# Three-pass projections of a decoder step: the products with the low weight parts moved behind the others within a chunk

## The chip, the cores and the metric

One NeuronCore of a Trainium2 chip runs the whole program; the other cores are idle. The metric is the device time of one execution in microseconds (us), lower is better. TensorE (PE in the rows) multiplies into PSUM; ScalarE (ACT), VectorE (DVE) and GpSimdE (POOL) do the elementwise work; SyncE (SP) issues the DMAs.

## What is computed

One inference step of a small two-layer decoder, for 1024 prompt tokens and 8 x 4 sample tokens together (1056 columns). The part of the reference that matters here, cut:

```python
# layer 0 (self path)
h, s_fin = _hgrn2(_rmsnorm(x, a_norm), a_w_in, lbs, a_out_norm, a_w_out, state0, chunk, sub)
x = x + h
x = x + jnp.square(relu(_rmsnorm(x, mlp_norm[0]) @ mlp_w_up[0])) @ mlp_w_down[0]
# layer 1 (cross path)
kv = _rmsnorm(x, kv_norm) @ w_kv            # keys get a per-head norm and a rotary
q = _rmsnorm(x, b_norm) @ b_w_q             # 3 groups x 8 heads, the same norm and rotary
o = merge of three dilated attentions over (q, kv), weighted by their softmax denominators
x = x + o @ b_w_o
x = x + jnp.square(relu(_rmsnorm(x, mlp_norm[1]) @ mlp_w_up[1])) @ mlp_w_down[1]
```

`_hgrn2` projects q, f, i and og with `a_w_in` (1024 x 4096) and runs a gated recurrence with a 128 x 128 state per head.

## The kernel before

Everything is float32, and TensorE multiplies in its float32r form. Each operand of a product is held as a high part (`whi` for weights, `opH` for activations) and a low part, what is left of the value (`wlo`, `opL`). A product of weights and activations is three matmuls into the same PSUM bank: high x high (HH), high weight x low activation (HL), low weight x high activation (LH).

**Weights.** `weight_order` lists all weight tiles (128 x 1024 each) in the order of their use. `_prep` (lines 125 to 163) loads one with two DMAs of 256 KB into `wraw`; ScalarE copies each half into `whi` (L131), and GpSimdE subtracts it for `wlo` (L132). For the key, value and query weights GpSimdE first multiplies by a gain (L148). `whi` and `wlo` have two buffers each, so a tile's split waits until TensorE has done with the tile two before it. `wnext` prepares one tile ahead.

**Projections.** `mm3` (lines 180 to 189) is the helper of all projections but the MLP's second half (`mmx`, not touched). For one output tile of 128 rows and one chunk of columns it issues, for each of 8 blocks of the contraction (4 in the output projections), HH (L185), HL (L186) and LH (L187):

```python
for i, (kw, kx) in enumerate(ks):
    nc.tensor.matmul(ps, wh[:, kw, :], xh[:, kx, :], start=(i == 0), stop=False)
    nc.tensor.matmul(ps, wh[:, kw, :], xl[:, kx, :], start=False, stop=False)
    nc.tensor.matmul(ps, wl[:, kw, :], xh[:, kx, :], start=False, stop=(i == len(ks) - 1))
    if self.fine and 2 * i + 2 == len(ks):
        self.tick()
```

`proj_n` goes over three chunks (352 columns each in the first layer's mixer and the attention stage, 384, 384 and 288 elsewhere) and calls `mm3` and the evacuation of the bank, for one weight tile or, in the first projection and the first of the attention stage, for two in turn. `tick` lets one piece of a recurrence or an attention generator issue its instructions, after each chunk and, where `fine` is set, at half a chunk; so their small matmuls stand among the products. The order on each engine is that of a scheduler, which starts from the program's order and priorities (`high_priority`) and pulls forward what it takes to be ready.

**The start.** The input norm runs chunk by chunk (`norm`, lines 250 to 282): squares and their sum, a matmul with ones (L273), the reciprocal root on ScalarE (L239, L240), then for each of 8 blocks a multiply on VectorE (L281), the high part on ScalarE (L232) and the low part on GpSimdE or VectorE (L233). The first projection (f and q of head 0, banks `pj_226` and `pj_354` for chunk 0) follows it block by block.

**The attention stage.** `unit` projects a key tile (its squares on ScalarE, L1040, are summed by a matmul with ones, L1042), a value tile and four query tiles, for each of 2 x 3 units; attention runs between. Afterwards come the output projection and the second MLP.

Of the kernel before, what the change touches and what calls it, by code (L numbers as in the profile page):

```python
# [46 lines left out]
class Kern:  # L47
    def __init__(self, nc, tc, aps, ctx):
        self.nc, self.tc, self.a, self.ctx = nc, tc, aps, ctx
        self.const = ctx.enter_context(tc.tile_pool(name="const", bufs=1))  # L50
        self.rs = ctx.enter_context(tc.tile_pool(name="rs", bufs=2))
        self.op = [self.const.tile([P, KD, NT], F32R, name=n) for n in ("opH", "opL")]
        self.chunks = CHUNKS
        self.wp = ctx.enter_context(tc.tile_pool(name="wp", bufs=2))
        self.pp = ctx.enter_context(tc.tile_pool(name="pp", bufs=4, space=PSUM))
        self.pg = ctx.enter_context(tc.tile_pool(name="pg", bufs=4, space=PSUM))
        self.wx = None
        self.wt = {}
        self.wi = 0
        self.wq = self.weight_order()  # L60
        self.queue, self.lanes = deque(), []
        self.merged = 0
        self.every, self.ticks = 0, 0
        self.rawx = False
        self.fine = False

    def bank(self):
        return self.pg.tile([P, 512], F32, name="g")
# [111 lines left out]
    def mm3(self, ps, w, x, ks):  # L180

        nc = self.nc
        (wh, wl), (xh, xl) = w, x
        for i, (kw, kx) in enumerate(ks):
            nc.tensor.matmul(ps, wh[:, kw, :], xh[:, kx, :], start=(i == 0), stop=False)  # L185
            nc.tensor.matmul(ps, wh[:, kw, :], xl[:, kx, :], start=False, stop=False)  # L186
            nc.tensor.matmul(ps, wl[:, kw, :], xh[:, kx, :], start=False, stop=(i == len(ks) - 1))  # L187
            if self.fine and 2 * i + 2 == len(ks):
                self.tick()

    K8 = [(k, k) for k in range(KD)]
# [134 lines left out]
    def phase_a(self):  # L326
        nc, tc, a = self.nc, self.tc, self.a
# [38 lines left out]
        def ev_to(t):  # L366
            def ev(c, ps):
                with hp():
                    nc.scalar.activation(t[:, c * CW:(c + 1) * CW], ps, AF.Copy)
            return ev  # L370

        def sigmoid(x, mul):

            for c in range(NCH):
                x_ = x[:, c * CW:(c + 1) * CW]
                n = gp.tile([P, CW], F32, name="sg")
                nc.scalar.activation(n, x_, AF.Abs)
                nc.scalar.activation(n, n, AF.Exp, scale=-1.0)
                nc.scalar.activation(n, n, AF.Ln, bias=1.0)
                o = n if mul else x_  # L380
                nc.vector.scalar_tensor_tensor(o, x_, 0.0, n, op0=ALU.min, op1=ALU.subtract)
                nc.scalar.activation(o, o, AF.Exp)
                if mul:
                    nc.vector.tensor_tensor(x_, x_, n, op=ALU.mult)

        def ev_f(h, b, kt, lf):
            def ev(c, ps):
                sl = slice(c * CW, (c + 1) * CW)
                with hp():
                    f = gp.tile([P, CW], F32, name="fr")  # L390
                    nc.scalar.activation(f, ps, AF.Copy)
                n = gp.tile([P, CW], F32, name="fn", bufs=1)
                nc.scalar.activation(n, f, AF.Abs)
                nc.scalar.activation(n, n, AF.Exp, scale=-1.0)
                nc.scalar.activation(n, n, AF.Ln, bias=1.0)
                nc.vector.scalar_tensor_tensor(lf[:, sl], f, 0.0, n, op0=ALU.min, op1=ALU.subtract)
                nc.vector.scalar_tensor_tensor(n, f, 0.0, n, op0=ALU.max, op1=ALU.add)
                nc.scalar.activation(kt[:, sl], n, AF.Exp, scale=-1.0, bias=self.lnlb[:, h:h + 1])
                nc.vector.tensor_scalar(f, f, -80.0, None, op0=ALU.max)
                nc.scalar.activation(f, f, AF.Exp, scale=-1.0)  # L400
                nc.scalar.activation(f, f, AF.Ln, scale=self.lb[:, h:h + 1], bias=1.0)
                nc.vector.tensor_tensor(lf[:, sl], lf[:, sl], f, op=ALU.add)
                n, off = min(CW, NP_ - c * CW), c * CW % P
                nc.vector.tensor_tensor_scan(
                    b[:, c * CW:c * CW + n], self.reset[:, off:off + n], lf[:, c * CW:c * CW + n],
                    0.0 if c == 0 else b[:, c * CW - 1:c * CW], op0=ALU.mult, op1=ALU.add)
                if n < CW:
                    nc.vector.tensor_tensor_scan(b[:, NP_:], self.reset[:, 448:], lf[:, NP_:], 0.0, op0=ALU.mult, op1=ALU.add)

                for i in ((), (2, 3), (6, 7))[c]:  # L410
                    s = slice(i * P, i * P + P)
                    nc.vector.scalar_tensor_tensor(b[:, s], lf[:, s], b[:, s.stop - 1:s.stop], b[:, s], op0=ALU.add, op1=ALU.subtract)
            return ev

        def gate(h, og):
            self.proj(self.wnext(), ops, ev_to(og))
            sigmoid(og, False)
            nc.gpsimd.tensor_copy(self.so[:, h, :], og[:, NP_:])

        self.fine = True  # L420
        for h in range(8):
            b = gp.tile([P, NT], F32, name="b")
            kt = gp.tile([P, NT], F32, name="k")
            q = gp.tile([P, NT], F32, name="q")
            lf = gp.tile([P, NT], F32, name="lf", bufs=1)
            if h == 0:
                w = [self.wnext(), self.wnext()]
                self.proj_n(w, ops, [ev_f(h, b, kt, lf), ev_to(q)])
                for i in range(4):
                    mt = gp.tile([P, 512], F32, name="lv", bufs=6)[:, :480]  # L430
                    nc.sync.dma_start(mt, a["masks"][:, 480 * i:480 * i + 480])
                    nc.vector.tensor_copy(self.masks[:, 480 * i:480 * i + 480], mt)
            else:
                gate(h - 1, og)
                self.proj(self.wnext(), ops, ev_f(h, b, kt, lf))
                self.proj(self.wnext(), ops, ev_to(q))
            sigmoid(q, True)
            vT = gp.tile([P, NT], F32, name="vT", bufs=1)
            self.proj(self.wnext(), ops, ev_to(vT))
            if h % 4 == 0:  # L440
                new = [gp.tile([P, 4, NS], F32, name=f"s_{n}", bufs=1) for n in "bkqv"]
            for d, s in zip(new, (b, kt, q, vT)):
                nc.gpsimd.tensor_copy(d[:, h % 4, :], s[:, NP_:])
            og = gp.tile([P, NT], F32, name="og", bufs=1)
            self.queue.append(self.gla(h, b, kt, q, vT, og))
            if h == 3:
                self.lanes.append(self.gla_sample(0, new))
# [1074 lines left out]
```

## Time and profile before

| | |
|---|---|
| median of 3 runs | 2947.27 us (2946.01 to 2949.76) |
| the profiled execution's own time | 2947.01 us |
| its span | 2945.2 us |
| TensorE busy | 2853.4 us, 97% |
| VectorE / ScalarE / GpSimdE busy | 56% / 45% / 44% |
| moved by DMA | 201.90 MB, 69 GB/s on average |
| stages, about | recurrence to 620 us, MLP to 1415, attention and output to 2180, MLP to the end |

Matmuls overlap in the profile: a row's duration is longer than the distance to the next one's start. Waits in brackets are idle time just before an instruction, and what ended it.

### The profile page before, as it was taken

The numbers are of one execution on the slowest core, as the hardware profiler recorded it, in microseconds if no ns is written. First come the engines' busy times: TensorE is split into PE (matmuls) and PEld (weight loads), VectorE is DVE, ScalarE is ACT, GpSimd is POOL, SyncE is SP. The second block draws the span as 40 slices with busy tenths as digits, with TensorE's granted clock in tenths as the row PEclk, the third lists the DMA queues.
The fourth block names the chain that finished last, engine by engine and source line by source line (L and its number), as shares of the span: only waits on it lengthen the run. The fifth ranks groups of instructions, "written<-read, shape, count | busy, mean of one in ns | idle before, by whom it ended". The sixth has DMA issues, their size and how long they took to land.

```text
span 2945.2 us, 47177 instructions
## 1 busy us (share of the span) xinstructions
PE 2853.4 (97%) x18144; PEld 2747.6 (93%) x18144; DVE 1663.9 (56%) x3353; ACT 1330.1 (45%) x3045; POOL 1308.9 (44%) x1119
## 2 busy tenths in 40 slices
PE   6999999999999999999899999999999999999999
PEld 6999899889999999999889889889889999999999
DVE  8777777864454445443745555665675454444442
ACT  6676667743333322332445545555544233333221
POOL 5444454542554445453564454333214454544442
PEclk9999999999999999999999999999999999999999
DMA  3111211230111111112312234332651111111112
GB/s 117 38 31 37 74 38 34 88 102 29 51 44 51 44 51 47 48 51 70 94 44 77 73 102 119 127 116 70 196 165 44 51 44 50 51 44 50 44 51 88
DMA packets 131954, 201.90 MB, mean 69 GB/s; under 512 B 26321, under 2 KB 65873, under 8 KB 129681
## 3 DMA queue, kind: packets, MB, share of 16 engines
q1 hardware_dynamic: 131728, 198.88, 21.7%
q8 instruction: 143, 2.34, 0.3%
q14 instruction: 83, 0.67, 0.1%
HBM read 164.04 MB, written 34.80 MB: 68 GB/s over the span
## 4 chain that ended last, share of the span: by engine, by line
PE 60%; POOL 10%; DVE 7%; DMA 5%; issue 5%; ACT 3%; POOLq 0%; DVEq 0%; ACTq 0%; SPq 0%
PE pj L185 11%; PE pj L186 11%; PE pj L187 11%; POOL wlo L132 5%; PE pj L853 4%; PE pj L854 4%; PE pj L855 4%; DMA wraw<-w_dn 4%; POOL wlox L132 2%; PE g L854 2%; PE g L853 2%; PE g L855 2%; PE g L1195 2%; PE g L1167 2%; PE g L1182 1%
## 5 line engine op out<-in xcount | busy, mean ns | idle before, releaser
L185 PE MATMUL pj<-opH,whi 128*128 128x352 f32 (+2 forms) x3408 | 1134.7, 333 | 6.0 <-ACT opH L232 3.5
L186 PE MATMUL pj<-opL,whi 128*128 128x352 f32 (+2 forms) x3408 | 1107.2, 325 | 1.6 <-POOL opL L233 1.3
L187 PE MATMUL pj<-opH,wlo 128*128 128x352 f32 (+2 forms) x3408 | 1102.9, 324 | 3.0 <-POOL wlo L132 2.7
L132 POOL TENSOR_TENSOR wlo<-wraw,whi 128x512 fp32r<-128x512 f32 x404 | 546.4, 1372 | 976.6 <-ACT whi L131 939.8
L185 PEld LDWEIGHTS pj<-opH,whi 128*128 128x128 f32 x3408 | 644.6, 189 | 24.7 <-issue 13.7
L186 PEld LDWEIGHTS pj<-opL,whi 128*128 128x128 f32 x3408 | 645.3, 189 | 11.4 <-issue 5.2
L187 PEld LDWEIGHTS pj<-opH,wlo 128*128 128x128 f32 x3408 | 644.2, 189 | 7.0 <-POOL wlo L132 4.2
L131 ACT ACTIVATE whi<-wraw 128x512 fp32r<-128x512 f32 x404 | 233.0, 622 | 561.7 <-PE g L854 442.7
L767 DVE SCALAR_TENSOR_TENSOR tmp<-pj,scale 128x384 f32<-128x384 f32 (+1 forms) x192 | 99.8, 520 | 302.8 <-PE pj L187 302.8
L867 DVE TENSOR_TENSOR xr<-xr,pj 128x384 f32<-128x384 f32 x336 | 184.4, 552 | 143.4 <-PE pj L855 143.3
L768 ACT ACTIVATE tmp<-tmp 128x384 f32<-128x384 f32 (+1 forms) x192 | 94.8, 494 | 290.3 <-DVE tmp L767 289.5
L536 POOL TENSOR_TENSOR lv<-b 128x512 f32<-128x512 f32 x112 | 127.9, 1156 | 80.1 <-PE g L640 43.1
L132 POOL TENSOR_TENSOR wlox<-wsum,whix 128x512 fp32r<-128x512 f32 x112 | 151.4, 1373 | 0.0
L162 POOL TENSOR_TENSOR wsum<-wraw,wsum 128x256 f32<-128x256 f32 x56 | 41.4, 739 | 170.8 <-DVE wsum L160 166.5
L1172 ACT ACTIVATE pr<-pr,nm 128x128 f32<-128x128 f32 (+1 forms) x192 | 84.1, 440 | 65.9 <-DVE nm L1170 65.7
L1169 DVE CUSTOM_DVE_ANT_0 pr<-g,band,rq 128x128 f32<-128x128 f32 (+1 forms) x192 | 68.0, 404 | 77.2 <-PE g L1167 73.5
L148 POOL TENSOR_TENSOR wraw<-wraw,gains 128x512 f32<-128x512 f32 x72 | 92.1, 1284 | 42.2 <-DMA wraw<-w_q 34.8
L211 DVE TENSOR_TENSOR xr<-xr,pj 128x384 f32<-128x384 f32 (+1 forms) x132 | 67.5, 516 | 75.1 <-PE pj L855 38.1
L773 DVE TENSOR_TENSOR tmp<-tmp 128x384 f32<-128x384 f32 x84 | 80.5, 984 | 46.5 <-ACT tmp L768 46.5
L1019 POOL TENSOR_TENSOR q<-q,cos 32x512 f32<-32x512 f32 x48 | 89.3, 1866 | 29.8 <-DVE rsw L1018 28.5
L854 PE MATMUL g<-hL,whi 128*128 128x288 f32 x336 | 99.8, 297 | 0.0
L853 PE MATMUL g<-hH,whi 128*128 128x288 f32 x336 | 98.9, 294 | 0.0
(400 smaller groups left out, 5714.1 us busy)
## 6 DMA issues: line engine op xcount, KB each, us to landing
wraw<-w_up SPq DMA_DIRECT2D x128, 256.0 KB, 2.9
wraw<-w_dn SPq DMA_DIRECT2D x128, 256.0 KB, 2.8
wraw<-w_in SPq DMA_DIRECT2D x64, 256.0 KB, 2.8
wraw<-w_q SPq DMA_DIRECT2D x48, 256.0 KB, 3.0
ub<-us SPq DMA_DIRECT2D x32, 256.0 KB, 2.2
cc<-ck SPq DMA_DIRECT2D x8, 1024.0 KB, 4.9
cc<-cv SPq DMA_DIRECT2D x8, 1024.0 KB, 5.2
wraw<-w_kv SPq DMA_DIRECT2D x24, 256.0 KB, 2.9
```

What stands on the lines that cost most here:

```text
L131: nc.scalar.activation(hi[:, j:j + 4, :], raw, AF.Copy)
L132: nc.gpsimd.tensor_tensor(lo[:, j:j + 4, :], raw, hi[:, j:j + 4, :].bitcast(F32), op=ALU.subtract)
L185: nc.tensor.matmul(ps, wh[:, kw, :], xh[:, kx, :], start=(i == 0), stop=False)
L186: nc.tensor.matmul(ps, wh[:, kw, :], xl[:, kx, :], start=False, stop=False)
L187: nc.tensor.matmul(ps, wl[:, kw, :], xh[:, kx, :], start=False, stop=(i == len(ks) - 1))
L536: nc.gpsimd.tensor_tensor(r(lv), r(b), r(b)[:, :, h - 1:h].to_broadcast([P, 256 // h, 2 * h]), op=ALU.subtract)
L767: nc.vector.scalar_tensor_tensor(r, ps, 0.0, self.scale[c], op0=ALU.max, op1=ALU.mult)
L768: nc.scalar.activation(r, r, AF.Square)
L853: nc.tensor.matmul(ps, wh[:, kw, :], xh, start=start and i == 0, stop=False, skip_group_check=True)
L854: nc.tensor.matmul(ps, wh[:, kw, :], xl, start=False, stop=False, skip_group_check=True)
L855: nc.tensor.matmul(ps, wl[:, kw, :], xh, start=False, stop=stop and i == len(items) - 1, skip_group_check=True)
L867: self.nc.vector.tensor_tensor(x(i, c), x(i, c), ps, op=ALU.add)
```

## The change

Within one call of `mm3` the products are listed in two passes. The first has HH and HL for each block in turn; the second has LH for all blocks. The first product of the list starts the bank and the last one stops it. The tick in the middle still falls after half of the products. The attribute `fresh` is set and cleared and nothing reads it.

```diff
         (wh, wl), (xh, xl) = w, x
-        for i, (kw, kx) in enumerate(ks):
-            nc.tensor.matmul(ps, wh[:, kw, :], xh[:, kx, :], start=(i == 0), stop=False)
-            nc.tensor.matmul(ps, wh[:, kw, :], xl[:, kx, :], start=False, stop=False)
-            nc.tensor.matmul(ps, wl[:, kw, :], xh[:, kx, :], start=False, stop=(i == len(ks) - 1))
-            if self.fine and 2 * i + 2 == len(ks):
+
+        hh, hl, lh = (wh, xh), (wh, xl), (wl, xh)
+        passes = ((hh, hl), (lh,))
+        todo = [(f, kw, kx) for p in passes for kw, kx in ks for f in p]
+        for i, ((f, g), kw, kx) in enumerate(todo):
+            nc.tensor.matmul(ps, f[:, kw, :], g[:, kx, :], start=(i == 0), stop=(i == len(todo) - 1))
+            if self.fine and 2 * i + 2 == len(todo):
                 self.tick()
```

Two places of TensorE's order. In the changed program all products have line 190, the norm's matmul L273 is L276, and L1042 is L1046.

The first is in the first projection, from the product of chunk 0, block 6 on. `pj_226` and `pj_354` are chunk 0 of the two weight tiles (`whi_89` and `whi_103`), `pj_380` and `pj_421` chunk 1. Before:

```order
L185 MATMUL pj_226<-opH_61,whi_89 128x352
L186 MATMUL pj_354<-opL_62,whi_103 128x352
L187 MATMUL pj_354<-opH_61,wlo_104 128x352
L185 MATMUL pj_380<-opH_61,whi_89 128x352
L185 MATMUL pj_421<-opH_61,whi_103 128x352
L186 MATMUL pj_380<-opL_62,whi_89 128x352
L187 MATMUL pj_380<-opH_61,wlo_90 128x352
L185 MATMUL pj_380<-opH_61,whi_89 128x352
L273 MATMUL g_317<-og_145,onesD_73 128x352
L186 MATMUL pj_226<-opL_62,whi_89 128x352
L187 MATMUL pj_226<-opH_61,wlo_90 128x352
```

The same place in the changed program:

```order
L190 MATMUL pj_226<-opH_61,whi_89 128x352
L190 MATMUL pj_380<-opH_61,whi_89 128x352
L190 MATMUL pj_421<-opH_61,whi_103 128x352
L190 MATMUL pj_380<-opL_62,whi_89 128x352
L190 MATMUL pj_380<-opH_61,whi_89 128x352
L190 MATMUL pj_380<-opL_62,whi_89 128x352
L276 MATMUL g_317<-og_145,onesD_73 128x352
L190 MATMUL pj_226<-opL_62,whi_89 128x352
L190 MATMUL pj_226<-opH_61,whi_89 128x352
L190 MATMUL pj_226<-opL_62,whi_89 128x352
L190 MATMUL pj_226<-opH_61,wlo_90 128x352 x8
```

Ahead of the norm's matmul for chunk 2 there now stands a second product with `opL` of chunk 1 (block 1), which came later before; the products with `wlo` are gathered behind.

The second is a unit's key projection, where its third chunk (`pj_14520`) ends and the next one (`pj_14554`, a value tile's) begins. Before:

```order
L186 MATMUL pj_14520<-opL_62,whi_13807 128x352
L187 MATMUL pj_14520<-opH_61,wlo_13808 128x352
L185 MATMUL pj_14554<-opH_61,whi_14378 128x352
L186 MATMUL pj_14554<-opL_62,whi_14378 128x352
L187 MATMUL pj_14554<-opH_61,wlo_14379 128x352
L185 MATMUL pj_14554<-opH_61,whi_14378 128x352
L186 MATMUL pj_14554<-opL_62,whi_14378 128x352
L187 MATMUL pj_14554<-opH_61,wlo_14379 128x352
L185 MATMUL pj_14554<-opH_61,whi_14378 128x352
L186 MATMUL pj_14554<-opL_62,whi_14378 128x352
L187 MATMUL pj_14554<-opH_61,wlo_14379 128x352
L1042 MATMUL g_14547<-hsq_14545,onesH_75 128x352
```

The same place in the changed program:

```order
L190 MATMUL pj_14520<-opL_62,whi_13807 128x352
L190 MATMUL pj_14520<-opH_61,wlo_13808 128x352 x8
L190 MATMUL pj_14554<-opH_61,whi_14378 128x352
L190 MATMUL pj_14554<-opL_62,whi_14378 128x352
L190 MATMUL pj_14554<-opH_61,whi_14378 128x352
L190 MATMUL pj_14554<-opL_62,whi_14378 128x352
L1046 MATMUL g_14547<-hsq_14545,onesH_75 128x352
```

The last product that reads the high part of the key's weights now lies nine rows, not two, before the chunk's end, and the matmul that sums the squares stands behind four products of the next chunk, not nine. On ScalarE the two splits of the weights two tiles on (L131) still stand right ahead of the squares (L1040).

## Rows read from the trace of the kernel before

**Rows 1.** The page: the span, and each engine's busy time, share and instructions.

```profile
span 2945.2 us, 47177 instructions
...
PE 2853.4 (97%) x18144; PEld 2747.6 (93%) x18144; DVE 1663.9 (56%) x3353; ACT 1330.1 (45%) x3045; POOL 1308.9 (44%) x1119
```

**Rows 2.** Timeline of TensorE, 27 to 64 us: start, duration, instruction, idle before.

```profile
27.78 0.43 PE L185 MATMUL pj<-opH,whi 128*128 128x352 f32 x1
...
29.16 0.43 PE L186 MATMUL pj<-opL,whi 128*128 128x352 f32 x1 [0.31 <-DVE opL L233]
...
29.75 0.75 PE L273 MATMUL g<-og,onesD 128*128 128x352 f32 x2
...
33.53 0.43 PE L187 MATMUL pj<-opH,wlo 128*128 128x352 f32 x1 [1.78 <-POOL wlo L132]
...
35.86 0.49 PE L186 MATMUL pj<-opL,whi 128*128 128x352 f32 x1
...
48.60 0.43 PE L186 MATMUL pj<-opL,whi 128*128 128x352 f32 x1 [0.55 <-POOL opL L233]
...
54.64 0.43 PE L187 MATMUL pj<-opH,wlo 128*128 128x352 f32 x1 [0.95 <-POOL wlo L132]
...
59.24 0.32 PE L185 MATMUL pj<-opH,whi 128*128 128x352 f32 x1
...
63.71 0.32 PE L186 MATMUL pj<-opL,whi 128*128 128x352 f32 x1
```

**Rows 3.** Busy us by stretch: PE, PEld, DVE, ACT, POOL; clock, DMA.

```profile
900.00:1000.00 100.00, 99.59 (x621) 99.09 (x621) 47.77 (x88) 33.35 (x65) 47.21 (x40) 1.00 0.16 47
...
1400.00:1500.00 100.00, 90.61 (x559) 85.17 (x558) 66.31 (x98) 45.42 (x100) 61.84 (x49) 1.00 0.26 81
...
2100.00:2200.00 100.00, 93.23 (x625) 85.98 (x624) 70.36 (x223) 49.34 (x150) 15.36 (x12) 0.98 0.62 193
```

**Rows 4.** Instructions by line, TensorE: count, busy us, mean ns, idle before.

```profile
L185 PE MATMUL pj<-opH,whi 128*128 128x352 f32 (+2 forms) x3408 | 1134.7, 333 | 6.0 <-ACT opH L232 3.5 <-DVE xr L211 1.2 <-ACT opH L947 1.1
...
L185 PE MATMUL pj<-opH,whix 128*128 128x384 f32 (+1 forms) x96 | 31.5, 328 | 0.0
...
L185 PE MATMUL pj<-opH,q 128*128 128x384 f32 (+1 forms) x48 | 16.3, 339 | 0.0
```

**Rows 5.** The same by shape, 700 to 1300 us (first MLP).

```profile
L185 PE MATMUL pj<-opH,whi 128*128 128x384 f32 x464 | 157.4, 339 | 0.0
L186 PE MATMUL pj<-opL,whi 128*128 128x384 f32 x464 | 156.3, 337 | 0.0
L187 PE MATMUL pj<-opH,wlo 128*128 128x384 f32 x464 | 155.9, 336 | 0.0
```

**Rows 6.** Timelines of GpSimdE, ScalarE and VectorE at the start.

```profile
28.58 3.39 POOL L233 TENSOR_TENSOR opL<-lv,opH 128x352 fp32r<-128x352 f32 x2 [2.15 <-ACT opH L232]
...
38.53 1.21 POOL L233 TENSOR_TENSOR opL<-lv,opH 128x352 fp32r<-128x352 f32 x1 [1.49 <-ACT opH L232]
...
27.24 1.65 ACT L232 ACTIVATE opH<-lv 128x352 fp32r<-128x352 f32 x4
...
28.59 0.51 DVE L233 TENSOR_TENSOR opL<-lv,opH 128x352 fp32r<-128x352 f32 x1
```

**Rows 7.** Busy us by stretch, 34.5 to 37.8 us, columns as in rows 3.

```profile
34.50:37.80 3.30, 3.30 (x13) 3.19 (x12) 3.30 (x4) 1.73 (x4) 2.54 (x3) 0.50 0.25 76
```

**Rows 8.** Timelines of TensorE and ScalarE, end of a key projection.

```profile
1454.60 0.32 PE L186 MATMUL pj<-opL,whi 128*128 128x352 f32 x1
1454.76 0.32 PE L187 MATMUL pj<-opH,wlo 128*128 128x352 f32 x1
...
1456.52 0.86 PE L1042 MATMUL g<-hsq,onesH 128*128 128x352 f32 x2
...
1454.96 1.15 ACT L131 ACTIVATE whi<-wraw 128x512 fp32r<-128x512 f32 x2 [1.15 <-PE pj L186]
1456.02 0.44 ACT L1040 ACTIVATE hsq<-pj 128x352 f32<-128x352 f32 x1
```

**Rows 9.** Who waited for whom, ScalarE, 1420 to 2180 us: us, times, longest.

```profile
ACT whi L131 <- PE pj L186: 62.0, 32, 3.8
```

More of the change, by code (lines that the diff above doesn't have):

```diff
@@ L65, in __init__ @@
         self.fine = False
+        self.fresh = True
     def bank(self):
@@ L428, in phase_a @@
                 self.proj_n(w, ops, [ev_f(h, b, kt, lf), ev_to(q)])
+                self.fresh = False
                 for i in range(4):
```

## The prediction

> **What bounds the kernel now.** I read the page's table of engines first. TensorE is busy for 97% of the span [rows 1]. Its matmuls overlap, so that share alone says little. The timeline says more: away from the start, 28 products of 352 columns begin one after the other in 4.47 us, 0.16 us each, with no gap [rows 2], from 59.24 to 63.71. Next come the busy times by stretch of 100 us: 99.6 us of TensorE in the middle of an MLP, 90.6 us where the MLP gives way to the attention stage, 93.2 us near the end of that stage [rows 3]. So in the MLPs nothing is to be won by waiting less; time can go only where a matmul costs more or less, or at a few places in the start and in the attention stage. Third, I followed each of these in the timelines of the engines.
>
> The profiled execution took 2947.0 us (span 2945.2 and 1.8 around it), 0.3 below the median of the runs shown. The sum is made against 2947.0.
>
> **What the change moves.** The projection helper issues 3 x (3408 + 96 + 48) = 10,656 products [rows 4], before and after: the same operands, bank and weight load for each. Per chunk of 8 k-blocks the order was HH, HL, LH for each k (weights' part first, operand's second); it becomes HH, HL for all k and then eight LH. The array takes new weights equally often: twice per k. The mid-chunk tick still falls after half of the products.
>
> *Cost of the products themselves: 0.* In the undisturbed MLP stretch the three kinds have means of 339, 337 and 336 ns at 384 columns [rows 5], though each stands in a different place of the triple; that is what speaks for a cost that knows no neighbour. The ends come from the same rows: if the low products rise to the HH mean, 3 ns x 3552 = +10.7 us; if HH and HL fall to the LH mean, (3 + 1) ns x 3552 = -14.2 us.
>
> The Trainium skill (TensorE: Matmul & The Clock Gate, section Back-to-back issue gap) gives a spacing of N/2.4 + 2.5 ns, an estimate of 149 ns at 352 columns, and says that in a stream of weight loads and matmuls both set it; the rows give 160 ns. By that page 11 ns of each product would be caused by what stands around it, and if order were the cause, up to 10,656 x 11 ns = 117 us could be at stake. The trace does not agree that order is the cause: the kinds differ by 3 ns.
>
> *The first projection.* Before, TensorE waits 1.78 and 0.95 us for low parts of weights and 0.31 and 0.55 us for low parts of operands [rows 2]. Now the low weights are wanted later, so the first two waits should go. But in the first pass the operands are used up in two products per k, not three, and TensorE has less to do while ScalarE, VectorE and GpSimdE make them. The order shows the place: the HL product of chunk 1, k = 1 now stands ahead of the norm's sum (L273) and of the rest of chunk 0. Step by step: the product of 27.78 runs then in both, since its operand comes from ScalarE [rows 2, 6]. The HL product of chunk 1, k = 0 still begins at 29.16, after VectorE's subtraction (28.59 + 0.51). One more product, and at 29.6 TensorE stands before an operand that is the second of GpSimdE's two subtractions of 28.58 + 3.39 = 31.97 [rows 6]. That is a **new wait of 2.4 us**; 1.78 us of wait goes for it. From 32.0: one product, L273 (0.3), then 27 products of 0.16 to the end of chunk 0, at 36.8. Before, that point is reached at 35.86 [rows 2], so +0.9. Before, TensorE then ran at 1.2 GHz for a while after its wait (granted clock 0.50 from 34.5 to 37.8: 13 products in 3.3 us, where 0.16 us each would give 20.7, so 1.2 us lost) [rows 7]; 0.7 of that falls behind 35.86. If the low clock does not come back: +0.9 - 0.7 = +0.2, then 1.2 us of wait for the last operand of chunk 1 (GpSimdE, 38.53 + 1.21 = 39.74 [rows 6], while the twelfth product from 36.8 is due at 38.6): +1.4. If it does: +0.9 + 1.2 - 0.7 = +1.4, and then no wait, since TensorE is too late for one. Both give +1.4. After that the waits of 0.55 and 0.95 us go: TensorE is later, ScalarE's queue now has the root for the third chunk (L240) ahead of two evacuations, not behind them, and the low weights are wanted 16 products later. **-0.1 us**. Ends: +1.4 if neither of the two later waits goes; -4.8 if the new waits cost nothing, all four go (3.6) and the low clock too (1.2).
>
> *ScalarE's queue in the attention stage.* ScalarE splits weights into the buffer that TensorE has just left: L131 twice, then L1040, the square that the next small matmul L1042 wants. Before, the weight's last HL product starts at 1454.60, L131 at 1454.96, L1040 at 1456.02, and L1042 runs at 1456.52, after nine products of the next chunk and 0.16 us of wait [rows 8]. Now the last read of the high part lies eight products before the chunk's end: 1453.48 instead of 1454.60. L131 would run from 1453.84 to 1454.99, L1040 from 0.36 after the chunk's last product, 1455.12 to 1455.56. And the scheduler has put L1042 behind four products, not nine: due at 1455.56. The wait would be 0.06: 0.1 us won. There are six such units: **-0.6 us**. Ends: -1.0 (all waits go); +4.8, if L1040 does not come earlier, and L1042 stands 0.8 us longer at each of the six.
>
> *What else is moved, at 0.* GpSimdE makes wlo as late as before where it waits for a buffer, which the last product frees in both orders. From 60 to some 570 us and between 620 and 1415 us TensorE's sequence of other matmuls among the products is unchanged. In the last recurrence (570 to 620 us) and the attention stage some small matmuls, evacuations, stores and cache loads on SP trade places by a few rows; TensorE covers them, and its idle time of 9.4 and 6.8 us in the two worst stretches [rows 3] is the most that they could give or, doubled, take.
>
> **The sum:** 2947.0 - 0.1 - 0.6 = **2946.3 us**, with ends at 2941.2 and 2953.2. I forecast no change that can be measured.
>
> **The rivals.**
> *ScalarE's queue frees more.* In the attention stage ScalarE waits 62.0 us in 32 waits for TensorE to let go of a high part [rows 9]; each gets up to eight products (1.3 us) shorter, and whatever stands behind L131 comes sooner. For: TensorE is idle 16.2 us in the two stretches of [rows 3]. Against: ScalarE is far from full there, and most of what TensorE waits for in them is made by VectorE or late norms. If half of that idle time goes: -8 us, 2938.3.
> *The products get slower* (the other side). Eight LH in a row need new weights for every product, where the old order gave a product with kept weights between; if the low products then take as long as HH does, +10.7 us: 2957.0. It decides from 1.7 ns per low product (5.9 us over 3552). For: HH, which always follows a change of weights, has the longest mean. Against: LH follows such a change too and has the shortest.
> *The products get faster*, by the reverse: -14.2 us, 2932.1.
> *The change does not do what it says for ScalarE*: L131 waits for something other than the high buffer; +4.8 us, 2951.7. This is within the forecast's own range.
>
> **How the numbers follow.** 0.2% of the time, 5.9 us, is about what a measurement can tell from no change. Forecast (with the last rival in it) 0.68: no change. ScalarE frees more 0.15 and products faster 0.05: faster by over 0.2%, 0.20. Products slower 0.12: slower. The range leaves out the two cases of the products (0.17) and reaches to the others: 2938 to 2954.
>
> **What would show it.** In the changed profile, right: no wait of an LH product for wlo in the first 60 us; a wait of 2 to 2.5 us of the product on opL near 29.6, and L273 near 32; each L131 in the attention stage about 1.1 us earlier against its chunk's end, with L1042 waiting 0.1 us or less; products 0.16 us apart throughout. Wrong: a spacing other than 0.16 in the long MLP stretch (the product rivals), or the attention stage shorter by several us (ScalarE's queue), or L1042 waiting 0.8 us at each unit.

## The result and the profile after

Before: 2948.52 us, median of 4 runs (2946.01 to 2950.37). With the change: 2978.76 us, median of 4 (2976.95 to 2980.44). The ratio is 1.0099, 95% interval 1.0087 to 1.0112: **slower by 30 us**, where no measurable change was forecast (2946.3, 2938 to 2954). The profiled execution of the changed kernel has a span of 2976.9 us, 31.7 more than before. Its page:

```profile
span 2976.9 us, 47253 instructions
...
PE 2865.3 (96%) x18144; PEld 2760.2 (93%) x18144; DVE 1689.3 (57%) x3353; ACT 1322.1 (44%) x3045; POOL 1299.9 (44%) x1119
```

It answers to [rows 1] and tells nearly nothing: the same 18144 matmuls, one point less of busy share. What is needed is where the time went, and for that a landmark that both traces have. VectorE's evacuation of the up projections (L767 before, L771 after) occurs in the two MLPs only. The view of one line's instructions gives its first and last start. Before, first and second MLP:

```profile
L767 DVE SCALAR_TENSOR_TENSOR tmp<-pj,scale x96: 443/556/560, 707.1 to 1378.0; 128x384 f32<-128x384 f32 x64, 128x288 f32<-128x288 f32 x32
L767 DVE SCALAR_TENSOR_TENSOR tmp<-pj,scale x96: 442/556/559, 2228.0 to 2898.0; 128x384 f32<-128x384 f32 x64, 128x288 f32<-128x288 f32 x32
```

After:

```profile
L771 DVE SCALAR_TENSOR_TENSOR tmp<-pj,scale x96: 444/557/560, 713.0 to 1392.3; 128x384 f32<-128x384 f32 x64, 128x288 f32<-128x288 f32 x32
L771 DVE SCALAR_TENSOR_TENSOR tmp<-pj,scale x96: 444/557/559, 2254.2 to 2929.0; 128x384 f32<-128x384 f32 x64, 128x288 f32<-128x288 f32 x32
```

Subtracted, this is a ledger of the two profiled executions. The mixer costs 5.9 us (707.1 to 713.0). The first MLP takes 679.3 us and not 670.9, +8.4. From there to the second MLP, which is mainly the attention stage, 861.9 and not 850.0, +11.9. The second MLP 674.8 and not 670.0, +4.8. Behind it 0.7. The sum is 31.7. The loss is everywhere, and the MLPs, which the prediction set aside as full, have 13.2 of it. The MLPs' times repeat well from trace to trace, those of the other two stages do not, as the experiments below show; what the change costs there is better read from e5 and e6, 7 and 8 us.

**The MLPs.** The view of who waited for whom, TensorE, whole run, before and after:

```profile
PE pj L853 <- DVE xr L867: 7.4, 15, 0.9
```

```profile
PE pj L857 <- DVE xr L871: 21.9, 14, 2.3
```

A matmul of the down projection waits for an addition to `xr`: 14.5 us more, and 14 times, which is once for each of the 2 x 7 groups. One such place in VectorE's timeline (start, duration, instruction, idle before). Before:

```profile
852.74 0.54 DVE L867 TENSOR_TENSOR xr<-xr,pj 128x384 f32<-128x384 f32 x1
853.38 0.55 DVE L867 TENSOR_TENSOR xr<-xr,g 128x384 f32<-128x384 f32 x1
853.85 0.55 DVE L867 TENSOR_TENSOR xr<-xr,pj 128x384 f32<-128x384 f32 x1
854.68 0.55 DVE L867 TENSOR_TENSOR xr<-xr,pj 128x384 f32<-128x384 f32 x1 [0.28 <-PE pj L855]
857.98 0.43 DVE L159 TENSOR_TENSOR wsum<-wraw 128x256 f32<-128x256 f32 x1 [2.75 <-DMA wraw<-w_dn]
```

After:

```profile
860.08 0.55 DVE L871 TENSOR_TENSOR xr<-xr,pj 128x384 f32<-128x384 f32 x1
860.73 0.55 DVE L871 TENSOR_TENSOR xr<-xr,g 128x384 f32<-128x384 f32 x1
861.20 0.55 DVE L871 TENSOR_TENSOR xr<-xr,pj 128x384 f32<-128x384 f32 x1
866.18 0.43 DVE L160 TENSOR_TENSOR wsum<-wraw 128x256 f32<-128x256 f32 x1 [4.43 <-DMA wraw<-w_dn]
866.52 0.55 DVE L871 TENSOR_TENSOR xr<-xr,pj 128x384 f32<-128x384 f32 x1
```

And TensorE after:

```profile
864.45 0.34 PE L859 MATMUL pj<-hbH,wlo 128*128 128x384 f32 x1
867.12 0.45 PE L857 MATMUL pj<-hpH,whix 128*128 128x384 f32 x1 [2.33 <-DVE xr L871]
```

Before, VectorE does four additions and then the first sum of raw weights (`wsum`, for a tile that is wanted two tiles later), which has to await its DMA. After, it does three, and the fourth stands behind `wsum`. That addition reads an accumulator that a product further on goes on writing, so this product has to wait for it. Its data were there some 4 us earlier (the product that it reads started at 861.80); its queue was not free. The products themselves stand in the same order on TensorE here: `down` isn't touched by the change.

The Trainium skill (PSUM — Partial Sum Buffer, section Engine vs sequencer instructions) says that the queues of ScalarE, VectorE and GpSimdE are strict FIFO. The trace agrees: VectorE stood idle 4.43 us with a ready addition second in line.

**The attention stage.** The same pattern on ScalarE, at one place. Before (ScalarE's timeline):

```profile
1878.37 0.40 ACT L1172 ACTIVATE pr<-pr,nm 128x128 f32<-128x128 f32 x1 [1.43 <-DVE nm L1170]
...
1879.92 0.68 ACT L1327 ACTIVATE mo<-mu,mc 128x128 f32<-128x128 f32 x2
```

After:

```profile
1899.81 0.69 ACT L1331 ACTIVATE mo<-mu,mc 128x128 f32<-128x128 f32 x2 [2.98 <-DMA mu<-ub]
1900.41 0.39 ACT L1176 ACTIVATE pr<-pr,nm 128x128 f32<-128x128 f32 x1
```

`mo`, a piece of a merge that waits for a load, has moved ahead of the softmax exponentials `pr`, for which TensorE then waits 3.14 us (4.6 us in 3 waits over the stage, against 2.7 us in 3). All of TensorE's waits in this stage add up to 30.1 us before (1410 to 2180 us) and 33.0 after (1425 to 2206): this alone does not make the stage's loss.

**The recurrence.** Its largest wait is for the masked copy to `A` on VectorE; whole run, before and after:

```profile
PE g L554 <- DVE A L558: 3.8, 5, 1.5
```

```profile
PE g L558 <- DVE A L562: 11.0, 6, 2.8
```

Other waits shrank, though: together TensorE's waits are 28.2 us before (60 to 620 us) and 30.5 after (60 to 626).

**The clock.** The mean granted clock of the span is 0.991 after and 0.995 before. A stretch of time T at clock c loses at most (1 - c) x T against full speed. The lower of the two levels (1.2 GHz, shown as 0.50) stands for 27 us of the trace before and 55 us of the one after, so at most 14 and 28 us are lost to it: some 14 of the 31.7 us. By stage (cut at the landmarks), the lower level stands for 17 us of the mixer before and 27 after, for 10 and 24 us between the MLPs, for none and 3 us in them. Half of the difference is 5 of the mixer's 5.9 us and 7 of the 11.9 between the MLPs. The busy times agree. The mixer, then the stretch between the MLPs, each before and after (columns as in [rows 3]):

```profile
0.00:707.10 707.10, 657.50 (x4178) 622.92 (x4179) 528.74 (x994) 462.83 (x1075) 326.65 (x330) 0.99 0.19 60
0.00:713.00 713.00, 660.54 (x4175) 626.64 (x4176) 522.05 (x993) 461.02 (x1073) 325.09 (x330) 0.98 0.19 59
1378.00:2228.00 850.00, 818.64 (x5413) 753.95 (x5412) 512.52 (x1214) 437.52 (x1144) 342.05 (x248) 0.99 0.34 106
1392.30:2254.20 861.90, 827.93 (x5422) 762.20 (x5422) 515.09 (x1215) 441.44 (x1144) 340.26 (x248) 0.99 0.34 105
```

TensorE's idle time, a stretch's length less PE's busy time, grew by only 2.9 and 2.6 us. So in the MLPs the loss is waiting; in the other two stages of these two traces more than half of it is matmuls that run at the lower clock. Two stretches at that clock in the changed kernel, which begin in a wait of TensorE, at the start and in the attention stage:

```profile
30.40:37.20 6.80, 5.62 (x17) 5.12 (x18) 5.90 (x7) 2.62 (x7) 4.78 (x4) 0.50 0.15 39
...
1453.80:1460.60 6.80, 6.09 (x19) 5.59 (x20) 3.95 (x8) 2.78 (x6) 1.83 (x2) 0.50 0.13 46
```

### The profile page after: what moved, and what is told of

Read it like the earlier page. It is cut to its first block, busy times and chain, and to the rows that moved or that the text cites. A ratio compares the mean times of both kernels' runs of the same rounds, so it can differ in the third digit from the quotient of the medians.

```text
span 2976.9 us, 47253 instructions
## 1 busy us (share of the span) xinstructions
PE 2865.3 (96%) x18144; PEld 2760.2 (93%) x18144; DVE 1689.3 (57%) x3353; ACT 1322.1 (44%) x3045; POOL 1299.9 (44%) x1119
## 4 chain that ended last, share of the span: by engine, by line
PE 66%; POOL 9%; DVE 9%; DMA 6%; issue 6%; ACT 3%; SPq 0%; POOLq 0%; DVEq 0%; ACTq 0%
PE pj L190 37%; POOL wlo L133 4%; PE pj L857 4%; PE pj L858 4%; PE pj L859 4%; DMA wraw<-w_dn 4%; PE g L858 2%; PE g L857 2%; PE g L859 2%; POOL wlox L133 2%; PE g L1199 2%; PE g L1171 1%; PE g L558 1%; PE g L1186 1%; POOL wsum L163 1%
## 5 line engine op out<-in xcount | busy, mean ns | idle before, releaser
L190 PE MATMUL pj<-opH,whi 128*128 128x352 f32 (+2 forms) x3408 | 1121.5, 334 | 5.8 <-ACT opH L235 4.3
L133 POOL TENSOR_TENSOR wlo<-wraw,whi 128x512 fp32r<-128x512 f32 x404 | 539.8, 1356 | 972.9 <-ACT whi L132 728.5
L190 PE MATMUL pj<-opH,wlo 128*128 128x352 f32 (+2 forms) x3408 | 627.0, 324 | 0.0
L190 PEld LDWEIGHTS pj<-opH,wlo 128*128 128x128 f32 x3408 | 563.1, 189 | 1.8 <-issue 1.2
L771 DVE SCALAR_TENSOR_TENSOR tmp<-pj,scale 128x384 f32<-128x384 f32 (+1 forms) x192 | 100.1, 521 | 247.1 <-PE pj L190 246.9
L160 DVE TENSOR_TENSOR wsum<-wraw 128x256 f32<-128x256 f32 x56 | 28.3, 505 | 152.8 <-DMA wraw<-w_dn 152.8
L545 DVE TENSOR_TENSOR lv<-lv,q 128x256 f32<-128x256 f32 x112 | 73.9, 669 | 54.1 <-ACT lv L543 52.0
```

What stands on the lines that cost most here:

```text
L133: nc.gpsimd.tensor_tensor(lo[:, j:j + 4, :], raw, hi[:, j:j + 4, :].bitcast(F32), op=ALU.subtract)
L190: nc.tensor.matmul(ps, f[:, kw, :], g[:, kx, :], start=(i == 0), stop=(i == len(todo) - 1))
L771: nc.vector.scalar_tensor_tensor(r, ps, 0.0, self.scale[c], op0=ALU.max, op1=ALU.mult)
```

## The experiments

**Theory Q (queues).** The last chunk's last read of `whi` is eight products earlier, so the high weight buffer falls free earlier. The scheduler, which orders all engines' instructions in advance, then takes the preparation of weights to be ready earlier and pulls it forward. On VectorE and ScalarE something that waits for a DMA gets ahead of something that TensorE waits for. **Theory D (diffuse).** The reordered products themselves cost, wherever they stand, in proportion to their number.

Most kernels choose the order by a flag, set where the text says:

```diff
-        passes = ((hh, hl), (lh,))
+        passes = ((hh, hl), (lh,)) if self.byp else ((hh, hl, lh),)
```

Each group of runs was timed beside the kernel before on its own chip (medians 2948.6 to 2949.8; single executions there lay between 2944 and 2957). The ratios are the recorded ones; quotients of the medians differ from them by up to 0.1%. Stage times are from the landmark rows of each kernel's one profiled execution. Where the order is the old one and nothing is held, the MLPs' times agree within 1.2 us; the mixer's vary by 6 us (705.6 to 711.9), by 13 with the change's order (709.7 to 722.5), and the time between the MLPs by 7 (847.5 to 854.8). So differences of a few us in these two columns mean nothing.

| run | median us | ratio to before (95%) | mixer | MLP 1 | between | MLP 2 |
|---|---|---|---|---|---|---|
| before | 2948.5 | | 707.1 | 670.9 | 850.0 | 670.0 |
| the change | 2978.8 | 1.0099 (1.0087 to 1.0112) | 713.0 | 679.3 | 861.9 | 674.8 |
| e1 | 2961.8 | 1.0046 (1.0031 to 1.0061) | 706.4 | 677.8 | 852.9 | 675.1 |
| e2 | 2969.6 | 1.0075 (1.0060 to 1.0090) | 707.0 | 679.4 | 852.9 | 679.4 |
| e3 | 2961.5 | 1.0033 (1.0018 to 1.0048) | 722.5 | 667.9 | 860.6 | 665.6 |
| e4 | 2946.1 | 0.9990 (0.9981 to 0.9999) | 706.2 | 669.4 | 849.2 | 668.4 |
| e5 | 2956.6 | 1.0024 (1.0011 to 1.0036) | 709.7 | 671.4 | 847.5 | 669.8 |
| e6 | 2957.9 | 1.0028 (1.0017 to 1.0038) | 706.5 | 671.5 | 857.3 | 669.5 |
| e7 | 2949.8 | 1.0002 (0.9991 to 1.0014) | 710.5 | 670.7 | 851.8 | 669.7 |
| e8 | 2940.2 | 0.9972 (0.9962 to 0.9983) | 708.1 | 668.5 | 847.7 | 665.7 |
| e9 | 2957.4 | 1.0028 (1.0018 to 1.0037) | 713.1 | 672.0 | 851.4 | 673.0 |
| e10 | 2974.6 | 1.0088 (1.0073 to 1.0103) | 714.2 | 677.0 | 859.7 | 678.3 |
| e11 | 2952.0 | 1.0013 (1.0003 to 1.0023) | 710.8 | 669.0 | 855.9 | 670.4 |
| e12 | 2943.0 | 0.9986 (0.9976 to 0.9996) | 711.9 | 668.5 | 854.8 | 668.1 |
| e13 | 2955.3 | 1.0020 (1.0011 to 1.0028) | 714.6 | 671.2 | 847.9 | 670.7 |
| e14 | 2953.0 | 1.0008 (1.0000 to 1.0017) | 705.6 | 673.1 | 852.1 | 671.1 |
| e15 | 2955.6 | 1.0024 (1.0014 to 1.0033) | 712.5 | 671.2 | 852.0 | 670.1 |

**Which stage.** e1, e5 and e6 have the new order in one stage only: the flag is set around the two calls of `mlp`, from the start to the first of them, or around `phase_c`. e1:

```diff
+        k.byp = True
         k.mlp(0, ops, after)
+        k.byp = False
```

> New order in the MLPs' up projections only, the old order in every other projection. Theory Q (queue order): the loss in the MLPs is 14 waits of TensorE for a VectorE addition of the down projection that now stands behind an addition of weights (wsum) which waits for its transfer; the MLPs account for 17.8 us of the 31.6 us between the two traces, so 2948.5 + 17.8 = about 2966, with the wait for xr at about 22 us in 14 times. Theory D (every reordered chunk costs the same): 192 of the 444 chunks of products are in the MLPs, so 30.2 x 192/444 = 13.1 us, 2961.6. If the MLP's loss only came from being started later or with another queue state by the stages before: about 2948.5.

> New order only in the first layer's mixer (start, recurrence, its output projection), the old order from the first MLP on. In the traces TensorE in the changed kernel is 5.7 us later than in the one before where the mixer ends. Theory Q (the loss is made where it shows, by VectorE's and ScalarE's queues of that stage): 2949 + 5 to 7 = 2954 to 2956, and the waits on A (masks) near 11 us against 3.8. Theory D (every reordered chunk costs the same, 30.2 us over 444 chunks): the mixer has 132 of them, +9, 2958. If the 5.7 us were an accident of one execution's clock: 2949.

> New order only in the attention stage and its output projections. Theory Q: the stage itself loses, 10.5 us between the two traces, of which some 4 us are stretches at the low clock: 2949 + 6 to 10 = 2955 to 2959, with a wait of about 3 us on pr near the third unit and of 2 us on us. Rival: the loss of this stage is inherited from the mixer's changed queues (another offset between its DMAs and TensorE): then 2949.

+0.46%, +0.24% and +0.28% add up to 0.98%, against 0.99% for the change: each stage makes its own loss. e6 has the waits of the whole change in its stage (5.5 us for `pr`, 3.6 us for `us`), e5 those on `A` (13.6 us). That ends the idea that one stage passes its loss on to the next. It doesn't yet tell the theories apart. e1 has theory Q's waits (20.4 us for `xr`, 14 times), but came out at theory D's 2961.6 and not at theory Q's 2966, and per reordered chunk the three stages cost nearly the same (0.46% for 192 chunks, 0.24% for 120, 0.28% for 132; the expectations, here and below, give the mixer 132 chunks, but the trace before has 2880 products, 120 chunks, ahead of the first MLP).

e5 also shows what the mixer's loss is made of. Its profiled execution has those waits on `A` and took 2947.7 us, no longer than the kernel before, at a mean granted clock of 0.996; the longest of its ten took 2963.5 us, at 0.991. (1 - c) x T gives 15 of these 16 us. So the loss comes and goes with the clock, in executions of one program. The mean clock of the ten is 0.993, that of the kernel before beside them 0.996, which is 8 us; e5 lost 7. For e6 the same sum gives 3 of its 8 us (0.995 against 0.996); the other 5 are not placed one by one.

**Is it the products, or what the scheduler does with them?** e2 sets the flag for one up projection of four in each group:

```diff
+                self.byp = j == 0
                 self.proj(self.wnext(), ops, evs[j])
+                self.byp = False
```

> New order in one up projection of four in each group of the MLPs (the one that precedes the down projections), the old order in all others; in the built order this alone turns VectorE's row of four additions, wsum into three additions, wsum, addition in all 14 groups. Theory Q: nearly the whole loss of the MLPs, 2948.5 + 14 to 18 = 2963 to 2966, with 14 waits of 1.5 to 2.4 us for xr. Theory D: 48 of 444 chunks, 30.2 x 48/444 = 3.3 us, 2951.8.

Theory D is far off: +0.75% for 48 chunks, more than e1 pays for all 192 (why more is not shown; theory Q's 2966 is 4 us short too). The waits:

```profile
PE pj L858 <- DVE xr L872: 23.7, 15, 1.9
```

e3 goes the other way: every product as in the change, and only `wsum` held back by a false dependency (the copy reads what the fifth addition, that of the third chunk, writes; the column it writes is overwritten at once; `two` holds the tile's number in its group):

```diff
+                if two[0] == 2:
+                    nc.vector.tensor_copy(t[:, 0, :1], self.xr[:, 0, self.chunks[2]][:, :1])
                 tt(t[:, :2], a21, a22, op=ALU.add)
```

> The changed kernel with every product in the new order; one thing added: in the third weight tile of each group's down projections the first wsum addition is held back behind the fourth xr addition and the fifth (one tiny copy of VectorE, 14 times, some 0.1 us each). Theory Q: the 14 waits shrink to at most the 0.9 us of before, so 2978.8 - 14.5 = about 2964, at most 2967. Theory D: no better than the changed kernel, 2978 to 2981.

2961.5, in the expected range; the wait is down to

```profile
PE pj L859 <- DVE xr L873: 3.5, 9, 0.8
```

and both MLPs are shorter than before the change (667.9 and 665.6). So **the MLPs' loss is this one place in VectorE's queue**: e2 makes it with a quarter of the reordered products, e3 mends it with all of them. The 11 us by which e3 is still slower than the kernel before lie in the other stages, and the clock alone can account for them: its five executions have a mean of 0.991, those of the kernel before beside them 0.9955, which is 13 us.

e10 and e11 ask the same of the whole program. The flag is set in `proj_n`; e11 has `c < NCH - 1` in its place. The output projections have the old order in both.

```diff
+                self.byp = c == NCH - 1
                 self.mm3(ps, w, ops[c], self.K8)
+                self.byp = False
```

> New order only in the last of the three chunks of each weight tile (projections with eight blocks), 3168 of 10,656 products; the old order elsewhere. Only the last chunk decides when the high buffer falls free. Theory Q: nearly the whole loss, 2949 + 25 to 30 = 2974 to 2979. Theory D: 30.2 x 3168/10656 = 9 us, 2958.

> The complement: new order in the first two chunks of each weight tile, 6336 of 10,656 products, the old order in the last chunk, where the buffer is released. Theory Q: 2949 within 2 us. Theory D: 30.2 x 6336/10656 = 18 us, 2967.

As theory Q has it: 3168 products in the last chunks cost 0.88%, 6336 in the others 0.13%. So the number of reordered products doesn't decide; whether the last read of the buffer moves does. e11 is over its 2 us (0.13% is 4 us, interval 1 to 7), and why is not shown.

**Is the release all?** e9 leaves the new order and puts only the last read back:

```diff
         todo = [(f, kw, kx) for p in passes for kw, kx in ks for f in p]
+        todo.append(todo.pop(2 * len(ks) - 1))
```

> The changed kernel with one product of each chunk put back: the HL product of the last block stands behind the eight LH products, so that TensorE's last read of the high weight buffer is at the chunk's end again. All others stay in the new order. In the built program this leaves VectorE's queue at 86 rows that differ from the kernel before, against 745 for the change. Theory Q (the early release of the high buffer lets the scheduler hoist the preparation of weights and so shuffles the other engines' queues): the whole loss goes, 2949 within 3 us, no wait of over 1 us for xr. Theory D (the reordered products themselves cost, wherever they stand): 2978 as the changed kernel. If the release explains the MLPs alone: 2949 + 15 = 2964.

0.28%: 21 of the 29 us go, 8 stay, where theory Q said none. The wait for `xr`, which was to stay under 1 us each, is not quite back at the 7.4 us of before either:

```profile
PE pj L858 <- DVE xr L872: 9.9, 18, 1.4
```

e13 and e14 split this kernel by stage (the line above only where the flag is set), e7 and e15 the change itself within the mixer: the flag is on up to the end of the first projection in e7, and from there to the first MLP in e15.

```diff
                 self.proj_n(w, ops, [ev_f(h, b, kt, lf), ev_to(q)])
-                self.fresh = False
+                self.byp = True
```

> The order of e9 (new, with the last HL product at the chunk's end) in the first layer's mixer only, the old order from the first MLP on. If e9's remaining 8 us are made in the mixer (its start has new waits for low operands, and its queues differ by the most rows): 2949 + 5 to 8 = 2954 to 2957. If they are spread over the reordered products: 132 of 444 chunks, +2.5, 2951.5.

> The complement: the order of e9 in both MLPs and the attention stage, the old order in the mixer. If the 8 us are the mixer's: 2949 within 2 us. If they are spread over the products: 312 of 444 chunks, +5.9, 2955.

> New order in the first projection alone (f and q of head 0, 6 chunks), the old order in all others: the one step that the prediction worked out row by row. By that working -0.1 us; in the trace of the changed kernel TensorE is at most 5.5 us late in it and even again where it ends (-0.1). So 2949, within 2 us; the new wait of 2.4 us on opL must show. If the low clock that follows it costs beyond it: up to +3, 2952.

> The new order in the mixer but for its first projection, the old order from the first MLP on. The new order in the first projection alone gave 0 (e7) and in the whole mixer 7 us (e5). If the recurrence's queues make the mixer's loss: 2949 + 6 to 7 = 2955 to 2956, with 10 us or more of wait on A (masks). If start and recurrence only lose together: within 2 us of 2949.

e13: +0.20%, e14: +0.08%. Most of the rest is the mixer's. There two stretches tell which part. e13, busy times by stretch:

```profile
0.00:100.00 100.00, 76.20 (x413) 69.94 (x414) 80.11 (x130) 68.45 (x158) 51.57 (x50) 0.95 0.31 97
350.00:615.00 265.00, 251.95 (x1642) 238.72 (x1642) 204.89 (x398) 185.94 (x436) 131.15 (x136) 0.99 0.17 52
```

e15, the same:

```profile
0.00:100.00 100.00, 76.21 (x434) 70.07 (x435) 84.50 (x133) 70.69 (x163) 52.10 (x51) 0.98 0.31 97
350.00:615.00 265.00, 249.76 (x1605) 238.02 (x1605) 200.65 (x393) 178.93 (x422) 127.62 (x134) 0.97 0.17 52
```

In e15 the recurrence (350 to 615 us) gets through 1605 matmuls and has the lower clock; in e13, with the release put back, 1642, as before the change (1644), at 0.99. This holds in all traces: 1600 to 1625 matmuls in these 265 us where the last read of the last chunk moves in the recurrence (the change, e3, e5, e10, e15), 1636 to 1646 in the other twelve. So the recurrence's loss goes with the release too, though not by the waits on `A`: e13 still has 10.5 us of them, the kernel before 4.8. Whether it is the order of the queues or the earlier release itself that does it in the recurrence and the attention stage, no run separates. What e13 keeps it keeps elsewhere, and the start is where its clock is lower (0.95; before 0.98). It also has a wait there that neither the change nor e7 shows, and e9 does:

```profile
PE pj L192 <- ACT whi L132: 1.7, 1, 1.7
```

That the start makes up all of e13's 6 us is not shown: the new order in the first projection alone (e7) costs nothing that can be measured, with the same 0.95 at its start. Of e9's 8 us, these 1.7 and the 2.5 us more of wait for `xr` have a place in its trace; the rest stays open. e14, at 0.08%, lies between its two expectations.

**A version that beats both.** If a `wsum` ahead of an addition costs time, so must the 7.4 us of the same wait in the kernel before. e4 (behind the sixth addition) and e12 (behind the fourth and the fifth, as e3) hold it back with the old order everywhere; e8 has the new order in the MLPs, with the hold of e3. e4's is:

```diff
+                if two[0] == 2:
+                    nc.vector.tensor_copy(t[:, 0, :1], self.xr[:, 1, self.chunks[1]][:, :1])
```

> The kernel before, old order everywhere, with the third weight tile's first wsum addition held back behind the sixth addition of the first down projection (one tiny copy, 14 times). Theory Q says that the remaining 15 waits of 7.4 us in all in the kernel before are of the same kind: they should go, 2948.5 - 5 to 7 = 2942 to 2944. If the later sums make the split weights late for their own down projection, it is slower: a wait for whix or wlox would show, 2950 or more.

> The kernel before, old order everywhere, with the hold of run e8 (wsum of the third weight tile behind the fourth addition and the fifth). If the gain of e8 comes from the hold alone: 2940, like it. If the new order in the MLPs adds to it: 2944 to 2946, between the kernel before and e8.

> New order in the MLPs only, and there the third weight tile's wsum held behind the first down projection's fourth addition and the fifth. Theory Q: both parts of the MLPs' waits for xr go, as in the held changed kernel, whose MLP stretches took 797.5 and 758.3 us against 799.9 and 761.6 before: 2949 - 5.7 = about 2943, below the kernel before. If the new order costs something in the MLPs that the hold does not mend: 2949 or more.

All three are faster than the kernel before: -0.10%, -0.14%, **-0.28%** (2940.2 us, interval 0.9962 to 0.9983). e4 stays 2 us short of what was expected, and 4.4 of the 7.4 us of wait are left in it; e12 falls between its two cases; e8 is 3 us better than expected. The wait in e8:

```profile
PE pj L858 <- DVE xr L872: 2.7, 9, 0.7
```

Whether the new order adds to the hold in e8 stays open: the intervals of e8 and e12 overlap. In the profiles the second MLP took 665.7 us in e8 and 665.6 in e3, both with the new order, and 668.1 in e12 without.

## Why the prediction was wrong

*The products cost 0*: right. The three kinds at 384 columns, 700 to 1300 us, after:

```profile
L190 PE MATMUL pj<-opL,whi 128*128 128x384 f32 x448 | 151.4, 338 | 0.0
L190 PE MATMUL pj<-opH,whi 128*128 128x384 f32 x448 | 151.2, 337 | 0.0
L190 PE MATMUL pj<-opH,wlo 128*128 128x384 f32 x448 | 87.8, 337 | 0.0
```

That is 337 to 338 ns, against 336 to 339 [rows 5]. These are durations, which overlap; the distances say the same. Eight LH of 352 columns in a row, and the product behind them:

```profile
1469.97 1.46 PE L190 MATMUL pj<-opH,wlo 128*128 128x352 f32 x8
1471.26 0.32 PE L190 MATMUL pj<-opH,whi 128*128 128x352 f32 x1
```

They take 1.29 us, 0.16 each, as in [rows 2]. And e11, with 6336 products in the new order, costs 4 us. Both rivals on the products fall. The reason given for slower products, a product that keeps its weights in the old order, was wrong by the trace before: it has 18144 weight loads for 18144 matmuls [rows 1], one for HL too. So does the 117 us fall that the prediction worked out from the Trainium skill (TensorE: Matmul & The Clock Gate, section Back-to-back issue gap) for the case that order sets the spacing: eight LH in a row are no dearer than an LH in a triple. The Trainium skill gives that formula for an isolated matmul there, and about 131 ns at 512 columns for a stream of weight loads and matmuls. The 160 ns measured here at 352 columns do not agree with the latter, and the 11 ns were no price that it puts on a product's neighbours.

*The first projection, -0.1*: right in its sum as far as can be measured, half right in its steps, and with some luck. After, TensorE's timeline:

```profile
31.58 0.66 PE L190 MATMUL pj<-opL,whi 128*128 128x352 f32 x1 [2.24 <-POOL opL L236]
32.04 1.38 PE L276 MATMUL g<-og,onesD 128*128 128x352 f32 x2
```

The new wait on `opL` is there (2.24 us, 2.4 predicted), L276 stands at 32.0 as worked out, and no product waits for `wlo` in the first 60 us. The low clock came back for 6.8 us, not 3.3 [rows 7]; the prediction priced a return, but at half this length. So chunk 0 ended at 39.4 us and not at 36.8, and TensorE was level with the kernel before only at 55 us (the 150th product starts at 55.03, before at 55.23). e7, the step by itself: 1.0002 (0.9991 to 1.0014).

*ScalarE's queue in the attention stage, -0.6*: right in kind, too small. ScalarE's wait of 62.0 us for TensorE's release of a high part [rows 9] fell to

```profile
ACT whi L132 <- PE pj L190: 33.6, 26, 2.6
```

and TensorE's wait for the squares (L1042 before, L1046 after) from

```profile
PE g L1042 <- ACT hsq L1040: 5.4, 3, 3.0
```

to

```profile
PE g L1046 <- ACT hsq L1044: 1.7, 3, 1.0
```

so 3.7 us are won there. Other waits of the same stage and its lower clock more than take them back. The rival that said ScalarE's queue frees more was right on ScalarE and wrong on the sum.

***What else is moved, at 0*: this step failed, and with it the forecast.** It said that from 620 to 1415 us TensorE's sequence of matmuls is unchanged, and took that for no change; and, ahead of it, that in the MLPs nothing is to be won by waiting less. The sequence is unchanged. But TensorE waits for VectorE there, and VectorE's sequence was not compared: 745 of its rows stand elsewhere in the changed program. In place of 0 the MLPs lost 13 us (e1: 0.46% of the time), by 14.5 us more of waits for `xr`. Of the recurrence and the attention stage the step said that TensorE covers a few traded places, with the idle time of two stretches, 16.2 us, as the bound. In place of that the mixer lost 0.24% and the attention stage 0.28% (e5, e6). The lower clock, a term that the sum had at the start only, makes up the mixer's 7 us and 3 of the attention stage's 8; idle time bounds neither. A stage that is 99% busy was read as one that can't lose; no busy share bounds a loss. The prediction had the cause in its hands: it worked out that the last read of `whi` moves by eight products, and followed that to ScalarE in one stage, where it helps. It didn't ask what a scheduler that sees an earlier release does with the other two engines.

The case on the other side that the prediction gave (slower products) named a mechanism that these runs don't show. The range ended 25 us short.

## What to carry to other kernels

Where a scheduler fixes every engine's order in advance, moving the last read of a buffer on one engine can reorder the queues of all: compare the queues of each engine that the bound engine waits for before putting "the rest" at 0. In such a queue look for an instruction that waits for a transfer and stands ahead of one that frees an accumulator or feeds the bound engine; a one-column copy as a false dependency holds it back for next to nothing, and won 3 to 4 us in the kernel before. When the order of products must change but nothing else should, keep the last read of each buffer where it was.

## What the runs showed of the hardware that was not expected

Waits of TensorE of the same length are followed by the lower clock in one trace and not in another. At the entry to the attention stage (60 us), the kernel before, then e4, which has the same products there, then the changed kernel:

```profile
1415.00:1475.00 60.00, 50.61 (x307) 47.49 (x306) 40.73 (x56) 25.95 (x57) 37.15 (x30) 1.00 0.37 115
```

```profile
1413.00:1473.00 60.00, 52.53 (x301) 49.07 (x301) 39.07 (x56) 25.57 (x56) 35.78 (x30) 0.94 0.36 112
```

```profile
1430.00:1490.00 60.00, 53.34 (x299) 49.97 (x298) 43.46 (x56) 26.04 (x57) 36.21 (x30) 0.91 0.36 115
```

The waits for the norm's sum in the three stretches are 5.0, 5.0 and 5.5 us (longest 2.8, 2.8 and 3.2), and the clock is 1.00, 0.94 and 0.91; e3, with 5.4 us (longest 3.1), has 1.00. By (1 - c) x T the lower clock takes up to 3.6 and 5.4 us in the last two. So a sum that counts a wait at its own length may be short by as much again, and a single profiled execution doesn't tell by how much: e5's ten executions of one program lie 16 us apart, at clocks from 0.996 to 0.991.
